# A two-layer mixer network in float32 on one core: loads of x moved to ScalarE's DMA queue, level tables of the recurrent branch made later

## The chip, the cores and the metric

The kernel runs on one core of one Trainium2 chip. The metric is the device time of one execution in microseconds (us); lower is better. The core has five engines that run their own instruction streams in order and meet by semaphores: TensorE (PE, matmuls; its weight loads are listed as PEld), VectorE (DVE), ScalarE (ACT), GpSimd (POOL) and SyncE (SP, which here only issues DMAs). DMAs are also issued from other engines' streams; such an issue stands in that engine's order like any other instruction, with its waits.

## The reference

Two layers over x of 512 rows by 1024 columns, float32. Cut to what matters:

```python
def reference(x, w_in, ..., exp_w1, exp_w3, exp_w2):
    for layer in range(2):
        # p = x @ w_in, split into four branches and a gate:
        # sliding-window attention, RWKV-7 recurrence, forgetting attention, top-k sparse attention
        y = mixer_block(x, w_in[layer], ..., w_branch[layer], w_out[layer])
        x = layer_norm(DN_ALPHA * x + y, ln_g[layer, 0], ln_b[layer, 0])
        if layer == 0:
            y = swiglu(x, ffn_w1[0], ffn_w3[0], ffn_w2[0])
        else:
            y = moe_ffn(x, router_w[0], router_b[0], exp_w1[0], exp_w3[0], exp_w2[0])   # top 2 of 8
        x = layer_norm(DN_ALPHA * x + y, ln_g[layer, 1], ln_b[layer, 1])
    return x

# the recurrent branch, per head (in the kernel: chunks of 64 steps and an inverse of a triangular block)
state = state * w_t + (state @ -kk_t) (x) (kk_t * a_t) + v_t (x) k_t ;  y_t = state @ r_t
```

Each part of `p` and each gate is a projection of x, so before any of them x must be in the chip, transposed, on the contraction axis.

## The kernel before

**How it is tiled.** x is cut into four blocks of 128 rows (`TB = 4`), each in two halves of 512 columns, so x is eight tiles of 128 x 512 (256 KB); below they are x0 to x7. PE transposes each in four 128 x 128 pieces (line 228), ScalarE casts the result to the rounded high part `xh` (line 232) and VectorE subtracts to get the low part `xl` (line 233). Weights come the same way: a 512 KB DMA into `wraw` (two buffers), a ScalarE cast to `whi` (line 98), a VectorE subtraction to `wlo` (line 99; three buffers for each part). Every float32 product is then three matmuls: whi with xh (line 111), whi with xl (line 112), wlo with xh (line 113). An engine's order is fixed when the kernel is built: a scheduler takes instructions by priority, and code under `hot()` or `high_priority()` goes ahead of what stands around it; PSUM tiles have tags (`ps_mm` three buffers; `ps_s`, `ps_t`, `ps_o`, `ps_r`, `ps_y` one each).

**Loads of x.** `load_x` (lines 205 to 212) issues the eight DMAs from SyncE, line 211. It is called four times: at the start; in the merge of layer 0, where x is read again as the residual (about 440 us); at the end of the feed-forward layer (about 830 us); and in the merge of layer 1 (about 1519 us). In the first three the tiles are of the tag `pt`, which has seven buffers, so an eighth load waits until one is read; in the fourth they are of a tag with eight. SyncE's order holds the loads of weights as well (line 322 for `w_in`, 106 for the other matrices, 1382 and the like for the experts' `mwraw`).

**Completion of a DMA.** The scheduler gives every DMA that SyncE or ScalarE issues one of eight completion semaphores in turn, and a DMA waits until the DMA that had its semaphore before has landed. With the loads of x on two issuing engines, these waits cross between SyncE and ScalarE.

**Level tables.** `consts` builds masks on VectorE and GpSimd. Its last part makes `lev`, six masks of 128 x 64 used by the inverse in the recurrent branch (line 863; the uses in the trace start at 158.8 us). It makes integers `iq` and `jq` by shifts (lines 183 to 187), casts them (190, 191), and makes each level in three instructions (195 to 197). These tables lie in a pool that is closed after `consts`; its memory is used again later, among others by the state tiles `SD`, which GpSimd clears (line 804) before it clears a tile and writes it to the scratch buffer `inv` in memory by DMAs (`zero_inv`, lines 727 to 730).

Of the kernel before, what the change touches and what calls it, by code (L numbers as in the profile page):

```python
# [9 lines left out]
F32 = mybir.dt.float32  # L10
F32R = mybir.dt.float32r
BF16 = mybir.dt.bfloat16
I32 = mybir.dt.int32
AF = mybir.ActivationFunctionType
OP = mybir.AluOpType
# [3 lines left out]
P = 128  # L19
# [9 lines left out]
C = 64  # L29
# [27 lines left out]
class Net:  # L57
# [58 lines left out]
    def consts(self, tp):  # L116
        nc, cp = self.nc, self.const
# [50 lines left out]
        for r in range(2):  # L168
            s = self.ident64[64 * r:64 * r + 64]
            nc.gpsimd.affine_select(s, s, pattern=[[1, 64]], base=0, channel_multiplier=-1,  # L170
                                    compare_op=OP.is_equal, fill=0.0)

        self.lev = cp.tile([P, 6, 64], F32, name="lev")
        nc.vector.memset(self.lev, 0.0)
        ii = tp.tile([P, 1], I32, name="ii")
        jj = tp.tile([P, 64], I32, name="jj")
        nc.gpsimd.iota(ii, pattern=[[0, 1]], base=0, channel_multiplier=1)
        nc.gpsimd.iota(jj, pattern=[[1, 64]], base=0, channel_multiplier=0)
        iq = tp.tile([P, 2, 6], I32, name="iq")
        jq = tp.tile([P, 2, 6, 64], I32, name="jq")  # L180
        for l in range(6):

            nc.vector.tensor_scalar(iq[:, 0, l:l + 1], ii, l, 1, op0=OP.logical_shift_right, op1=OP.bitwise_and)
            nc.vector.tensor_scalar(iq[:, 1, l:l + 1], ii, 63, l + 1, op0=OP.bitwise_and,
                                    op1=OP.logical_shift_right)
            nc.vector.tensor_scalar(jq[:, 0, l], jj, l, 1, op0=OP.logical_shift_right, op1=OP.bitwise_and)
            nc.vector.tensor_scalar(jq[:, 1, l], jj, 63, l + 1, op0=OP.bitwise_and, op1=OP.logical_shift_right)
        iqf = tp.tile([P, 2, 6], F32, name="iqf")
        jqf = tp.tile([P, 2, 6, 64], F32, name="jqf")
        nc.vector.tensor_copy(iqf, iq)  # L190
        nc.vector.tensor_copy(jqf, jq)
        t = tp.tile([P, 64], F32, name="levt")
        for l in range(6):

            nc.vector.tensor_scalar(t, jqf[:, 0, l], -1.0, 1.0, op0=OP.mult, op1=OP.add)
            nc.vector.tensor_scalar(t, t, iqf[:, 0, l:l + 1], None, op0=OP.mult)
            nc.vector.scalar_tensor_tensor(self.lev[:, l], jqf[:, 1, l], iqf[:, 1, l:l + 1], t,
                                           op0=OP.is_equal, op1=OP.mult)
        self.reset = cp.tile([P, P], F32, name="reset")
        nc.vector.memset(self.reset, 1.0)  # L200
        nc.vector.memset(self.reset.rearrange("p (c t) -> p c t", t=C)[:, :, 0:1], 0.0)
        self.mhalf = cp.tile([P, 16], F32, name="mhalf")
        nc.vector.memset(self.mhalf, -0.5)


    def load_x(self, src):
        self.x = []
        for tb in range(TB):
            xt = [self.bt(self.xtag), self.bt(self.xtag)]
            for h in range(2):  # L210
                self.nc.sync.dma_start(xt[h], src[tb * P:(tb + 1) * P, h * 512:(h + 1) * 512])
            self.x.append(xt)

    def store_x(self, tb, dst):
# [133 lines left out]
    def mixer(self, layer):  # L348
        self.bp = self.sp
        self.o = {}  # L350
        pr = self.rwkv_proj(layer)
        if layer == 0:
            self.zero_inv()
        with self.hot():
            self.rwkv(layer, pr)
        self.v_proj(layer)
        self.forget()
        for g in range(2):
            q, = self.qk_split(layer, FOX0 + g * P, "qk", 1)
            k = self.dup_split(self.proj_b(layer, (FOX0 + 256 + g * P, P)))  # L360
            self.fox(g, q, k)
        sk = self.dup_split(self.proj_b(layer, (SWA0 + 512, P)))
        for kv in range(2):
            q = self.qk_split(layer, SWA0 + 256 * kv, "qk")
            self.swa(kv, q, sk[kv])
        iq = self.qk_split(layer, DSA0 + 384, "qk")
        k, ik = self.dup_split(self.proj_b(layer, (DSA0 + 256, 64), (DSA0 + 640, 64)))
        masks = self.index(iq, ik)
        self.dsa(self.qk_split(layer, DSA0, "rw"), k, masks)
        self.merge(layer)  # L370
# [1483 lines left out]
```

## Time and profile before

| | |
|---|---|
| Median of 3 runs | 2107.07 us (2104.9 to 2111.75) |
| The profiled execution's own time | 2107.6 us |
| Its span, first to last instruction | 2105.9 us |
| Mean granted TensorE clock | 0.988 of full speed |
| PE busy | 2019.7 us, 96% of the span |
| VectorE, ScalarE, GpSimd busy | 65%, 44%, 7% |

How to read it: a busy share is a mean over stages. PE idles 86.2 us in all (2105.9 - 2019.7), and most of this idle time lies in a few stretches. So the questions to ask of the trace are what PE waited for in the stretch that a change touches, and how long before PE needs it each other engine's result is there. Views used below: busy times of the whole span, busy times by stretches, sums of waits of PE, and timelines (each row: start, duration, engine, line, operation, out <- in, count, and in brackets how long the engine had been idle and what ended that).

### The profile page before, as it was taken

How to read it: one execution, taken by the hardware profiler on the slowest of the kernel's cores; microseconds unless marked ns; L12 is line 12 of the kernel's file. 1: busy time of each engine (PE TensorE's matmuls, PEld its weight loads, DVE VectorE, ACT ScalarE, POOL GpSimd, SP SyncE). 2: the span in 40 equal slices, each digit the busy share in tenths (PEclk: the TensorE clock that was granted, in tenths of full speed). 3: DMA queues.
4: the chain of work that ended last, by engine and by line, in shares of the span. 5: the costliest groups of instructions: out<-in, count | busy, mean ns of one | idle time of the engine just before them, and what ended most of it. 6: DMA issues, size and time to landing. Idle time of an engine off the chain costs nothing. (4 is left out here: it accounts for less than half of the span.)

```text
span 2105.9 us, 31148 instructions
## 1 busy us (share of the span) xinstructions
PE 2019.7 (96%) x11240; PEld 1569.9 (75%) x11240; DVE 1366.6 (65%) x2732; ACT 918.0 (44%) x1561; POOL 151.1 (7%) x211
## 2 busy tenths in 40 slices
PE   8999999999999999999999999999989999999994
PEld 7767777778888888888767778768877766677663
DVE  5677779844563333236676769844568877788778
ACT  3354543333232222113464553332326666677663
POOL 1020200000000000000011200000000000000043
PEclk9999999999999999999999999999999999999997
DMA  5231213343343334233221213313538988898872
GB/s 159 69 84 39 57 41 90 90 125 96 94 146 99 101 93 133 92 98 115 77 58 43 70 41 90 90 51 95 176 128 308 352 291 304 295 342 306 293 280 82
DMA packets 274976, 294.56 MB, mean 140 GB/s; under 512 B 23852, under 2 KB 203416, under 8 KB 274808
## 3 DMA queue, kind: packets, MB, share of 16 engines
q1 hardware_dynamic: 267736, 273.90, 40.2%
q0 software_dynamic: 7072, 18.49, 2.8%
q8 instruction: 97, 1.59, 0.3%
q14 instruction: 71, 0.58, 0.1%
HBM read 276.74 MB, written 15.60 MB: 139 GB/s over the span
## 5 line engine op out<-in xcount | busy, mean ns | idle before, releaser
L98 ACT CAST whi<-wraw 128x1024 fp32r<-128x1024 f32 (+1 forms) x218 | 228.1, 1046 | 625.4 <-PE ps_mm L112 376.9
L99 DVE TENSOR_TENSOR wlo<-wraw,whi 128x1024 fp32r<-128x1024 f32 (+1 forms) x218 | 265.5, 1218 | 361.2 <-ACT whi L98 355.0
L113 PE MATMUL ps_mm<-xh,wlo 128*128 128x512 f32 (+1 forms) x1288 | 494.9, 384 | 3.1 <-DVE rs L259 3.1
L111 PE MATMUL ps_mm<-xh,whi 128*128 128x512 f32 (+1 forms) x1288 | 496.5, 386 | 0.6 <-ACT whi L98 0.5
L112 PE MATMUL ps_mm<-xl,whi 128*128 128x512 f32 (+1 forms) x1288 | 492.1, 382 | 0.3 <-DVE xl L233 0.3
L113 PEld LDWEIGHTS ps_mm<-xh,wlo 128*128 128x128 f32 x1288 | 243.7, 189 | 49.8 <-DVE wlo L99 3.4
L111 PEld LDWEIGHTS ps_mm<-xh,whi 128*128 128x128 f32 x1288 | 243.8, 190 | 46.5 <-issue 2.6
L112 PEld LDWEIGHTS ps_mm<-xl,whi 128*128 128x128 f32 x1288 | 243.7, 189 | 45.8 <-issue 2.3
L1153 DVE TENSOR_TENSOR wlo<-mwraw,whi 128x1024 fp32r<-128x1024 f32 (+1 forms) x98 | 124.2, 1282 | 17.2 <-ACT whi L1152 16.0
L1152 ACT CAST whi<-mwraw 128x1024 fp32r<-128x1024 f32 (+1 forms) x98 | 95.9, 1005 | 16.0 <-PE ps_t L1503 10.1
L470 ACT COPY bt_pt<-ps_t 128x512 f32<-128x512 f32 (+2 forms) x80 | 41.7, 522 | 85.4 <-PE ps_t L467 84.6
L1153 DVE TENSOR_TENSOR mwlo<-mwraw,mwhi 128x1024 fp32r<-128x1024 f32 (+1 forms) x62 | 71.9, 1175 | 6.9 <-ACT mwhi L1152 6.4
L451 ACT ACTIVATE bt_pt<-ps_s,mx 128x256 f32<-128x256 f32 (+3 forms) x128 | 61.8, 487 | 21.8 <-DVE mx L445 18.0
L260 POOL TENSOR_TENSOR rs<-rs,mhalf 128x1 f32<-128x1 f32 x16 | 13.8, 861 | 724.2 <-DVE rs L259 724.2
L442 DVE TENSOR_REDUCE mx<-ps_s 128x2 f32<-128x512 f32 (+3 forms) x80 | 48.5, 607 | 22.1 <-PE ps_s L406 21.1
L1152 ACT CAST mwhi<-mwraw 128x1024 fp32r<-128x1024 f32 (+1 forms) x62 | 61.0, 999 | 3.2 <-DMA mwraw<-in_exp_w_dram 2.3
L1114 DVE TENSOR_TENSOR bt_pt<-bt_pt,ps_mm 128x512 f32<-128x512 f32 x22 | 15.1, 688 | 70.4 <-PE ps_mm L113 63.0
L467 PE MATMUL ps_t<-ident,bt_pt 128*128 128x128 f32 x272 | 51.5, 283 | 6.0 <-DVE bt_pt L461 4.8
L609 DVE MAX8 m<-bt_pt 128x8 f32<-128x256 f32 (+2 forms) x96 | 53.8, 560 | 2.7
L1153 DVE TENSOR_TENSOR wlo<-ring,whi 128x1024 fp32r<-128x1024 f32 (+1 forms) x45 | 51.5, 1160 | 2.5 <-DMA mwraw<-in_exp_w_dram 1.2
L610 DVE MATCH_REPLACE8 bt_pt<-m,bt_pt 128x256 f32<-128x256 f32 (+2 forms) x96 | 52.1, 543 | 0.0
L111 PE MATMUL ps_mm<-bt_o,whi 128*128 128x512 f32 x128 | 51.2, 400 | 0.4 <-ACT bt_o L511 0.4
(710 smaller groups left out, 4119.1 us busy)
## 6 DMA issues: line engine op xcount, KB each, us to landing
mwraw<-in_exp_w_dram SPq DMA_DIRECT2D x124, 512.0 KB
wraw<-in_w_in_dram SPq DMA_DIRECT2D x106, 512.0 KB
wraw<-in_ffn_w_dram SPq DMA_DIRECT2D x66, 512.0 KB
ring<-in_exp_w_dram SPq DMA_DIRECT2D x60, 512.0 KB
wraw<-in_exp_w_dram SPq DMA_DIRECT2D x32, 512.0 KB
mwraw<-in_exp_w_dram SPq DMA_DIRECT2D x36, 384.0 KB
wraw<-in_w_branch_dram SPq DMA_DIRECT2D x20, 512.0 KB
wraw<-in_w_out_dram SPq DMA_DIRECT2D x16, 512.0 KB
```

The costliest lines, as they stand in the source:

```text
L98: nc.scalar.copy(h, src)
L99: (low or nc.vector).tensor_sub(l, src, h.bitcast(F32))
L111: mm(ps, wh, xh, start=start, stop=False)
L112: mm(ps, wh, xl, start=False, stop=False)
L113: mm(ps, wl, xh, start=False, stop=stop)
L442: nc.vector.tensor_reduce(mx[:, 0:nh], s3, op=OP.max, axis=AX.X)
L451: nc.scalar.activation(p3[:, h], s3[:, h], AF.Exp, bias=nm[:, h:h + 1], scale=0.125, accum_out=mx[:, 4 + h:5 + h])
L467: nc.tensor.transpose(pt[:, i * P:(i + 1) * P], p3[:, h, kb * P:(kb + 1) * P], self.ident)
L609: nc.vector.max(m8, sc[:, :nk])
L610: nc.vector.match_replace(sc[:, :nk], m8, sc[:, :nk], REPL)
L1152: self.chain("hi", lambda: nc.scalar.copy(hi[:, :n], src))
L1153: self.chain("lo", lambda: nc.vector.tensor_sub(lo[:, :n], src, hi[:, :n].bitcast(F32)))
```

## The change

It has two parts. In `load_x` the DMA is issued from ScalarE (`nc.scalar.dma_start`) under `hot()`, at all four calls: 32 DMAs leave SyncE's order and stand in ScalarE's. And the part of `consts` that makes the level tables becomes a function of its own, `levels`, called in layer 0 after `rwkv_proj` and `zero_inv`. There `jq` and its float copy lie in four of the 28 buffers of the tag `rw`, and the copy is two casts in place of one. All line numbers from 205 on shift by up to 6.

```diff
@@ consts @@
         self.lev = cp.tile([P, 6, 64], F32, name="lev")
-        nc.vector.memset(self.lev, 0.0)
-        ii = tp.tile([P, 1], I32, name="ii")
-        jj = tp.tile([P, 64], I32, name="jj")
...
-        iq = tp.tile([P, 2, 6], I32, name="iq")
-        jq = tp.tile([P, 2, 6, 64], I32, name="jq")
...
-        nc.vector.tensor_copy(jqf, jq)
...
+    def levels(self):
+        nc = self.nc
+
+        nc.vector.memset(self.lev, 0.0)
+        ii = self.sp.tile([P, 1], I32, name="ii", bufs=1)
+        jj = self.sp.tile([P, 64], I32, name="jj", bufs=1)
...
+        iq = self.sp.tile([P, 2, 6], I32, name="iq", bufs=1)
+        jq = [self.bt("rw", I32)[:, 0:384].rearrange("p (l j) -> p l j", l=6) for _ in range(2)]
...
+        jqf = [self.bt("rw")[:, 0:384].rearrange("p (l j) -> p l j", l=6) for _ in range(2)]
+        nc.vector.tensor_copy(iqf, iq)
+        for a, b in zip(jqf, jq):
+            nc.vector.tensor_copy(a, b)
...
     def load_x(self, src):
...
             for h in range(2):
-                self.nc.sync.dma_start(xt[h], src[tb * P:(tb + 1) * P, h * 512:(h + 1) * 512])
+                with self.hot():
+                    self.nc.scalar.dma_start(xt[h], src[tb * P:(tb + 1) * P, h * 512:(h + 1) * 512])
...
@@ mixer @@
         if layer == 0:
             self.zero_inv()
+            self.levels()
```

ScalarE at the start of the program, before; the names are those of the section above.

```order
L98 ACT_TABLE_LOAD
L98 CAST whi<-wraw 128x1024 x2
L232 CAST xh<-ps_mm 128x4x128
L232 CAST xh<-ps_s 128x4x128
L232 CAST xh<-ps_mm 128x4x128
L98 CAST whi<-wraw 128x1024
L232 CAST xh<-ps_s 128x4x128
```

The same place after the change.

```order
L216 DMA bt_pt<-in_x_dram 128x512 x7
L98 ACT_TABLE_LOAD
L98 CAST whi<-wraw 128x1024 x2
L216 DMA bt_pt<-in_x_dram 128x512
L237 CAST xh<-ps_mm 128x4x128
L237 CAST xh<-ps_s 128x4x128
L237 CAST xh<-ps_mm 128x4x128
L237 CAST xh<-ps_r 128x4x128
L98 CAST whi<-wraw 128x1024
```

Seven loads of x now stand ahead of the table load and of both casts of weights, and the eighth behind these. The seventh waits for the landing of x0, the eighth for that of x1 and for PE's transposes of x0.

TensorE at the start, before.

```order
L228 MATMUL ps_mm<-ident,bt_pt 128x128 x4
L228 MATMUL ps_s<-ident,bt_pt 128x128 x4
L228 MATMUL ps_mm<-ident,bt_pt 128x128 x4
L228 MATMUL ps_r<-ident,bt_pt 128x128 x4
L228 MATMUL ps_s<-ident,bt_pt 128x128 x4
L111 MATMUL ps_mm<-xh,whi 128x256 x2
L112 MATMUL ps_mm<-xl,whi 128x256
```

After.

```order
L233 MATMUL ps_mm<-ident,bt_pt 128x128 x4
L233 MATMUL ps_s<-ident,bt_pt 128x128 x4
L233 MATMUL ps_mm<-ident,bt_pt 128x128 x4
L233 MATMUL ps_r<-ident,bt_pt 128x128 x4
L233 MATMUL ps_y<-ident,bt_pt 128x128
L111 MATMUL ps_mm<-xh,whi 128x256 x2
L233 MATMUL ps_y<-ident,bt_pt 128x128 x2
L233 MATMUL ps_s<-ident,bt_pt 128x128 x4
L233 MATMUL ps_y<-ident,bt_pt 128x128
L112 MATMUL ps_mm<-xl,whi 128x256
```

The first projection's matmuls now have one transpose of x5 (`ps_y`) ahead of them and seven more transposes, of x4 and x5, between the second and the third of them; before, twenty transposes of x0 to x4 stood ahead and those of x5 came later, at 18.10 us.

VectorE, a stretch in the middle of layer 0's projections, after the change: the level tables (lines 194 to 206) among the recurrent branch's preparation (649, 663, 782) and the weights' low parts (99). Before, no level instruction stands there; all lie ahead of line 295, in the first 22 us.

```order
L99 TENSOR_TENSOR wlo<-wraw,whi 128x912
L649 SCALAR_TENSOR_TENSOR bt_rw<-ps_mm,V,bt_rw 128x511
L194 TENSOR_SCALAR bt_rw<-jj 128x64
L195 TENSOR_SCALAR bt_rw<-jj 128x64
L194 TENSOR_SCALAR bt_rw<-jj 128x64
```

Here and in the rest of layer 0's mixer (about 50 to 420 us) the scheduler's order of PE, VectorE and ScalarE differs from before in many places; from there on it is the same but for the next place.

ScalarE in layer 1's merge, before.

```order
L98 CAST whi<-wraw 128x1024 x2
L1152 CAST mwhi<-mwraw 128x1024 x2
L98 CAST whi<-wraw 128x1024 x2
L1230 COPY xT<-ps_mm 128x512
L98 CAST whi<-wraw 128x1024
```

After.

```order
L98 CAST whi<-wraw 128x1024
L216 DMA bt_x<-xs_133 128x512 x8
L1158 CAST mwhi<-mwraw 128x1024
L98 CAST whi<-wraw 128x1024
L1158 CAST mwhi<-mwraw 128x1024
L98 CAST whi<-wraw 128x1024 x2
L1236 COPY xT<-ps_mm 128x512
```

All eight loads of x stand ahead of a cast of weights here, each with its wait for an earlier DMA. Their place in SyncE's order, behind the last `w_out` load, is empty now, and that load, and the constants behind it, wait for landings of x.

GpSimd at the start, after: the four clears of `SD` stand first, and the DMAs of `zero_inv` right behind the mask building, where before both stood behind a wait for the level tables.

## Rows read from the trace of the kernel before

**Rows 1.** The page: busy us, share of the span and instructions of each engine.

```profile
PE 2019.7 (96%) x11240; PEld 1569.9 (75%) x11240; DVE 1366.6 (65%) x2732; ACT 918.0 (44%) x1561; POOL 151.1 (7%) x211
```

**Rows 2.** By stretches: us, each engine's busy us (instructions), PEclk, DMA share, GB/s.

```profile
0.00:12.00 12.00, 5.06 (x22) 4.21 (x23) 8.20 (x46) 5.45 (x7) 3.82 (x21) 1.00 0.90 284
12.00:50.00 38.00, 37.71 (x233) 33.10 (x233) 19.75 (x45) 12.51 (x18) 3.42 (x8) 1.00 0.45 130
50.00:300.00 250.00, 241.07 (x1890) 180.95 (x1889) 176.85 (x535) 126.50 (x319) 34.16 (x51) 1.00 0.23 59
300.00:450.00 150.00, 148.60 (x722) 115.76 (x722) 121.83 (x272) 54.56 (x103) 0.00 (x0) 1.00 0.30 90
1010.00:1400.00 390.00, 376.92 (x2552) 285.71 (x2551) 290.87 (x800) 179.44 (x418) 33.33 (x50) 0.99 0.24 65
1508.00:1525.00 17.00, 17.00 (x76) 13.87 (x74) 8.63 (x22) 5.25 (x5) 1.37 (x7) 1.00 0.86 302
```

**Rows 3.** Waits of PE: who for whom, us in total, times, longest.

```profile
PE ps_mm L228 <- DMA bt_pt<-in_x_dram: 6.7, 1, 6.7
```

**Rows 4.** Line 211 over the whole run: ns min/median/max, first and last start.

```profile
L211 SPq DMA_DIRECT2D bt_pt<-in_x_dram x16: 327/431/1477, 1.9 to 581.7; - x16
```

**Rows 5.** Timeline of SyncE's queue, the start.

```profile
0.81 1.08 SPq L322 DMA_DIRECT2D wraw<-in_w_in_dram  x2
1.94 2.77 SPq L211 DMA_DIRECT2D bt_pt<-in_x_dram  x5
```

**Rows 6.** Timeline of ScalarE, the start.

```profile
0.81 1.28 ACT L98 ACT_TABLE_LOAD   x1 [0.81 <-PEq L1843]
4.46 1.04 ACT L98 CAST whi<-wraw 128x1024 fp32r<-128x1024 f32 x1 [2.36 <-DMA wraw<-in_w_in_dram]
5.95 1.05 ACT L98 CAST whi<-wraw 128x1024 fp32r<-128x1024 f32 x1 [0.45 <-DMA wraw<-in_w_in_dram]
7.87 0.58 ACT L232 CAST xh<-ps_mm 128x512 fp32r<-128x512 f32 x1 [0.88 <-PE ps_mm L228]
...
11.68 1.04 ACT L98 CAST whi<-wraw 128x1024 fp32r<-128x1024 f32 x1 [1.51 <-DMA wraw<-in_w_in_dram]
```

**Rows 7.** Timeline of TensorE, the start.

```profile
6.75 1.09 PE L228 MATMUL ps_mm<-ident,bt_pt 128*128 128x128 f32 x4 [6.75 <-DMA bt_pt<-in_x_dram]
7.63 1.06 PE L228 MATMUL ps_s<-ident,bt_pt 128*128 128x128 f32 x4
...
11.57 0.78 PE L111 MATMUL ps_mm<-xh,whi 128*128 128x256 f32 x2
```

**Rows 8.** Timeline of VectorE, the start.

```profile
9.25 0.68 DVE L233 TENSOR_TENSOR xl<-ps_mm,xh 128x512 fp32r<-128x512 f32 x1
...
21.64 0.29 DVE L197 SCALAR_TENSOR_TENSOR lev<-jqf,iqf,levt 128x64 f32<-128x64 f32 x1
```

**Rows 9.** Timeline of GpSimd, the start.

```profile
22.04 1.06 POOL L804 MEMSET SD<- 128x256 f32 x4 [16.79 <-DVE lev L197]
...
23.88 1.90 POOL L730 DMA_DIRECT2D inv<-bt_rw  x3 [0.31 <-POOL bt_rw L727]
```

**Rows 10.** Timeline of ScalarE, layer 0's merge and the feed-forward's end.

```profile
445.12 0.68 ACT L978 ACTIVATE gate<-ps_mm,V 128x512 f32<-128x512 f32 x1
451.09 1.05 ACT L98 CAST whi<-wraw 128x1024 fp32r<-128x1024 f32 x1 [5.28 <-issue]
...
840.48 1.05 ACT L98 CAST whi<-wraw 128x1024 fp32r<-128x1024 f32 x1 [4.23 <-PE ps_mm L1037]
```

**Rows 11.** Timeline of SyncE's queue, layer 1's merge.

```profile
1513.50 0.37 SPq L106 DMA_DIRECT2D wraw<-in_w_out_dram  x1
...
1519.40 4.78 SPq L211 DMA_DIRECT2D bt_x<-xs  x8
```

**Rows 12.** Timeline of ScalarE, the same stretch.

```profile
1513.76 1.05 ACT L1152 CAST mwhi<-mwraw 128x1024 fp32r<-128x1024 f32 x1 [1.55 <-DMA mwraw<-in_exp_w_dram]
...
1522.04 1.05 ACT L98 CAST whi<-wraw 128x1024 fp32r<-128x1024 f32 x1 [4.43 <-PE ps_mm L1037]
```

More of the change, by code (lines that the diff above doesn't have):

```diff
@@ L173, in consts @@
         self.lev = cp.tile([P, 6, 64], F32, name="lev")
-        nc.vector.memset(self.lev, 0.0)
-        ii = tp.tile([P, 1], I32, name="ii")
-        jj = tp.tile([P, 64], I32, name="jj")
-        nc.gpsimd.iota(ii, pattern=[[0, 1]], base=0, channel_multiplier=1)
-        nc.gpsimd.iota(jj, pattern=[[1, 64]], base=0, channel_multiplier=0)
-        iq = tp.tile([P, 2, 6], I32, name="iq")
-        jq = tp.tile([P, 2, 6, 64], I32, name="jq")
[L181 to L190, printed above, removed]
-        nc.vector.tensor_copy(jqf, jq)
[L192 to L198, printed above, removed]
         self.reset = cp.tile([P, P], F32, name="reset")
@@ L203, in consts @@
         nc.vector.memset(self.mhalf, -0.5)
+    def levels(self):
[3 more added lines that the diff above has]
+        jj = self.sp.tile([P, 64], I32, name="jj", bufs=1)
+        nc.gpsimd.iota(ii, pattern=[[0, 1]], base=0, channel_multiplier=1)
+        nc.gpsimd.iota(jj, pattern=[[1, 64]], base=0, channel_multiplier=0)
+        iq = self.sp.tile([P, 2, 6], I32, name="iq", bufs=1)
+        jq = [self.bt("rw", I32)[:, 0:384].rearrange("p (l j) -> p l j", l=6) for _ in range(2)]
+        for l in range(6):
+            nc.vector.tensor_scalar(iq[:, 0, l:l + 1], ii, l, 1, op0=OP.logical_shift_right, op1=OP.bitwise_and)
+            nc.vector.tensor_scalar(iq[:, 1, l:l + 1], ii, 63, l + 1, op0=OP.bitwise_and,
+                                    op1=OP.logical_shift_right)
+            nc.vector.tensor_scalar(jq[0][:, l], jj, l, 1, op0=OP.logical_shift_right, op1=OP.bitwise_and)
+            nc.vector.tensor_scalar(jq[1][:, l], jj, 63, l + 1, op0=OP.bitwise_and, op1=OP.logical_shift_right)
+        iqf = self.sp.tile([P, 2, 6], F32, name="iqf", bufs=1)
+        jqf = [self.bt("rw")[:, 0:384].rearrange("p (l j) -> p l j", l=6) for _ in range(2)]
+        nc.vector.tensor_copy(iqf, iq)
+        for a, b in zip(jqf, jq):
+            nc.vector.tensor_copy(a, b)
+        t = self.sp.tile([P, 64], F32, name="levt", bufs=1)
+        for l in range(6):
+            nc.vector.tensor_scalar(t, jqf[0][:, l], -1.0, 1.0, op0=OP.mult, op1=OP.add)
+            nc.vector.tensor_scalar(t, t, iqf[:, 0, l:l + 1], None, op0=OP.mult)
+            nc.vector.scalar_tensor_tensor(self.lev[:, l], jqf[1][:, l], iqf[:, 1, l:l + 1], t,
+                                           op0=OP.is_equal, op1=OP.mult)
     def load_x(self, src):
```

## The prediction, made before the change was run

> **What bounds the kernel now.** I read the page's busy times first. TensorE is busy 2019.7 us of the 2105.9 us span, VectorE 65%, ScalarE 44% [rows 1]; so an edit on the other engines moves the time only where it moves one of TensorE's waits. Then the busy times by stretches, to see where TensorE idles near the change [rows 2]. In the first 12 us it works 5.06 and waits 6.94; from 12 to 50 us it waits 0.29; in the rest of layer 0's mixer 250 - 241.07 = 8.93 from 50 to 300 us and 1.40 from 300 to 450 us. Third, the sums of TensorE's waits: loads of x hold it once, for 6.7 us, before its first transpose [rows 3]. The other three calls of `load_x` hold it for nothing. Last, the timelines of the four places where the loads are issued.
>
> So the change can gain at two places only: in the 6.94 us at the start, and in some 10 us of short waits in layer 0's mixer, which it doesn't aim at. At all others it can only lose.
>
> **The start.** Before, SyncE issues two weights, then five tiles of x [rows 5]; they land in that order: the first weight's cast starts at 4.46 us, the second's at 5.95 [rows 6], the first transpose at 6.75 [rows 7], and the third weight, whose issue stands behind the five tiles, is there at 11.68 [rows 6]. The second weight's 512 KB (524,288 bytes) took 5.95 - 4.46 = 1.49 us, 350 GB/s; over the first 12 us the DMA engines were busy 0.90 of the time at 284 GB/s [rows 2]. The loads are therefore held by the transfer of bytes, hardly by SyncE's issue (431 ns at the median, [rows 4]). Issuing x from ScalarE lets x start with the weights instead of behind them, and what one gains the other loses. At stake before the first projection matmul, at 11.57 us [rows 7], are both: it needs x0 and x2 cast, and ScalarE casts both weights before any tile of x, now as before. On top of that its order now has a transpose of x5 ahead of it.
>
> Step by step: the stream of bytes starts at about 4.46 - 1.49 = 3.0 us. If the two queues share evenly, two weights (1.05 MB) have come when as much of x has: 2.1 MB by 350 GB/s is 6.0 us, so the second weight is there at 9.0, not 5.95. Its cast takes 1.05 [rows 6], the eighth load's issue 0.43, three casts of x 0.58 each: 9.0 + 1.05 + 0.43 + 1.7 = 12.2 us. The other limit is x5: weights and six tiles are 2.62 MB, 7.5 us, so 10.5 us; but the four writes of `zero_inv` (1 MB), which now start at about 7 us and not at 23.88 [rows 9], since the wait of 16.79 us for the level tables ahead of them is gone, compete: up to 3.0 us more, 13.5. I take 12.9, the middle of 12.2 and 13.5. Work counts too. Before, twenty transposes stood ahead of the first matmul, now seventeen, and seven follow at once, where before four of these (x5's) came later; at about 0.21 us each (four from 6.75 to 7.63, [rows 7]) that is 3 x 0.21 = 0.6 us on the wrong side if the total is compared at the same point. So 12.9 - 11.57 + 0.6 = **+1.9 us**, and nothing behind it gives it back, since TensorE waits 0.29 us from 12 to 50 us.
>
> The bounds. Below: the weights keep 5.95 (they were issued at 0.81, with nothing before them), casts of x start at 7.4 and x5 lands at 10.5, at best 10.9 - 11.57 + 0.6, about 0. The `jq` shifts are also gone from ahead of the first `xl`, which started at 9.25 [rows 8] though its cast ended at 7.87 + 0.58 = 8.45 [rows 6]: 0.5 of these 0.8 at most, since TensorE had transposes to do. So -0.5. Above: x takes two thirds of the bytes until its seven tiles are there, and `zero_inv` its part: the second weight comes at 11.5, the first matmul at 15, +4.
>
> The Trainium skill (DMA: Bandwidth & Descriptors, section Queues, rings and completion order) says that a DMA engine turns in rotation between the queues that have work for it, a packet at a time, and that SyncE's and ScalarE's queues lie on the same 16 engines. That is the even share above; the trace of before, with one of the two in use, can't show it. By the same page's section Issuing engines are not separate DMA queues, the second issuer saves issue time alone; the rows with 0.90 busy agree.
>
> **The level tables.** Some 45 short instructions leave VectorE's first 22 us. The last ends at 21.93 [rows 8]; the first use is at 158.8 us. TensorE was busy all that time (0.29 us idle from 12 to 50 us), so nothing is saved but the 0.5 above. They go into the projections, where VectorE is 52% busy (19.75 of 38 us, [rows 2]), rising to 71% from 50 to 300 us; the tables cost it about 8 us there (six levels at 0.8 us, casts 0.7, shifts 2.4). Weights are split ahead of TensorE with three buffers for each part, so a delay of 0.3 us per level instruction is covered: 0. If the cover fails, a level or two (0.8 us each) stand ahead of a `wlo` TensorE waits for.
>
> But the scheduler laid out the whole mixer of layer 0 anew. What this does no row shows. The nearest is the same mixer in layer 1, laid out in another order again: it idles 390 - 376.92 = 13.1 us from 1010 to 1400, against 10.3 in layer 0 (8.93 + 1.40). So orders of one mixer differ by some 3 us. I take 0, with -4 to +5 as bounds (half of the idle time gone; one and a half times layer 1's surplus).
>
> **The loads in layer 0's merge and the feed-forward's end.** Eight issues at 0.43 us on ScalarE, 3.4 us. In the merge seven stand ahead of a cast of weights, and one waits for the end of the sparse attention. Replayed against the old times, ScalarE is through with the gate some 1.7 us later than 445.80, and is wanted next at 451.09 after 5.28 us idle [rows 10]. At the feed-forward's end the issues fall into gaps such as the 4.23 us before 840.48 [rows 10]. Both 0; if a landing that ScalarE waits for comes over 3.5 us later than I replay, TensorE waits for the rest.
>
> **The loads in layer 1's merge.** Here they come earlier, in ScalarE's order, and eight stand ahead of a cast of an expert's weights and of the third-last `w_out` cast. The last two of them wait for landings: of the second load of x, and of the first expert weight, which was there at 1513.76 [rows 12] without the competition. TensorE has no idle time there (17.00 of 17 us) and the DMA engines are 0.86 busy at 302 GB/s [rows 2], so 2 MB of x brought forward by some 8 us push others back by up to 2.1 / 0.3 = 7 us. Two things suffer. The `w_out` load issued at 1513.50 [rows 11] now waits for x to land, which I replay to about 1517; TensorE is through with the weight before it near 1522 (the cast at 1522.04 waited for that, [rows 12]). And the last one, before at 1518.99 ahead of x, now stands behind the constants. Against that VectorE may take x as soon as it is in. Cover: ScalarE idles 4.43 us before 1522.04 [rows 12]. A delay of 7 less the cover of 4.4 is 2.6, and part of it is regained as the 4.78 us of issue at 1519.40 [rows 11] is empty: I take **+1**, with -0.5 to +4 (the whole 7 us less half the cover).
>
> **Sum.** 1.9 + 0 + 0 + 1 = +2.9 on the profiled execution's 2107.6 us: 2110.5; it lies 0.5 above the median, so 2110.0. Bounds of all terms in one direction: -5 to +13; I keep the ends that go with one or two terms.
>
> **Rivals.** First, *the gain as meant*: the weights keep their places and x comes with them. For it: the weights are issued no later than now. Against it: bytes, 0.90 busy. -0.5 at the start, 0 to -1 elsewhere: 2106. Second, *the new order of the mixer wins*: 4 to 8 of the 10.3 us go, less the start's loss: 2107.1 - 6 + 1 = 2102, over to 2100 in few cases. For it, that VectorE's and GpSimd's start is free; against, that no wait of the mixer named a level table. Third, on the slower side, *ScalarE's order holds casts behind landings*: the seventh load waits for x0, the last of layer 1 for an expert's weight, while weights ready to be cast stand behind them. Its places are those without cover, the start (+4) and layer 1's merge (+4): 2107.1 + 8 = 2115. It decides from the point at which such a landing is later than 11.5 us at the start, or 1518 in layer 1's merge. Fourth, *the change doesn't do what it says*: x arrives no earlier because the engines, not the issue, set the rate, and no one waits: 2107.
>
> **How the numbers follow.** A measurement of this kernel can tell 0.3%, 6.3 us: 2100.8 to 2113.4 is no change. Forecast (+1 to +6) 0.50; gain as meant 0.12; no effect 0.10; a better mixer 0.12, of which 0.09 under 2100.8; ScalarE held 0.16, of which 0.15 above 2113.4, and 0.03 of the forecast's upper end with it. So faster 0.09, same 0.73, slower 0.18. The range that leaves out about 0.1 on either side is 2102 to 2117.
>
> **What would show it.** Right: the first projection matmul between 12 and 14 us, the second weight's cast near 9, not 5.95; the first transpose before 6; idle time from 50 to 450 us within 7 to 15; TensorE's waits at 440 to 455 and 825 to 960 unchanged; 0 to 4 us of new waits for `whi`, `wlo` or x between 1510 and 1540. Wrong: a first matmul before 11.5 (the queues don't share), idle time in layer 0's mixer under 6 or over 16 us (the order decides), or a cast of weights that ScalarE starts over 4 us late in layer 0's merge.

## The result, and the profile after

The changed kernel takes 2124.13 us at the median of 7 runs (2120.21 to 2128.41), the kernel before 2110.1 us in 7 runs (2104.9 to 2115.41). The ratio is 1.0058, with an interval of 1.0042 to 1.0075: about 12 us slower (the two medians lie 14 us apart). That lies outside the predicted range of 2102 to 2117. The profiled execution took 2124.1 us with a span of 2122.4, 16.5 more than before's; but before's profiled execution, 2107.6, is a low one among its own runs, so the difference of spans says a few us too much.

The page after, busy us of each engine, to be held against [rows 1]:

```profile
PE 2025.9 (95%) x11240; PEld 1571.3 (74%) x11240; DVE 1364.8 (64%) x2733; ACT 916.1 (43%) x1561; POOL 150.9 (7%) x211
```

Of the 16.5 us, 10.3 are idle time of TensorE (96.5 against 86.2) and 6.2 are busy time, with the same 11,240 matmuls. So some matmuls ran more slowly, and the cause of that has to be found as well.

**Where the time goes, by landmarks.** ScalarE casts every weight (`whi`; line 98, for the experts' weights line 1152), in the same number before and after. So I took the n-th such cast in both traces and subtracted the starts; the last column is the first cast of line 1152. The table gives this offset for the changed kernel and for all runs of the experiments below, in us; the first line is the cast's start in the kernel before. The last row is the kernel before, run again: its offsets show what can be read from such a table. They repeat within 0.14 us up to 936 us (0.35 over all casts there) and within 1.2 us up to 1575; behind that, in the mixture of experts, by up to 3.4 us.

| run | projections | 49.5 | end of mixer 0 | merge 0 | feed-forward's end | before merge 1 | behind merge 1 | ratio of times (95%) |
|---|---|---|---|---|---|---|---|---|
| before's start of it | 29.3 | 49.5 | 430.6 | 466.3 | 935.6 | 1500.2 | 1574.9 | |
| after | 4.66 | 4.66 | 2.69 | 12.62 | 12.44 | 12.58 | 15.50 | 1.0058 (1.0042 to 1.0075) |
| levels_only | 6.14 | 6.15 | 4.02 | 3.94 | 3.76 | 4.08 | 6.24 | 1.0004 (0.9994 to 1.0014) |
| loads_only | 3.83 | 12.88 | 17.20 | 26.51 | 26.52 | 26.52 | 32.44 | 1.0114 (1.0097 to 1.0131) |
| merge0_sp | 4.25 | 4.26 | 2.13 | 2.05 | 2.10 | 2.22 | 5.04 | 1.0015 (1.0001 to 1.0028) |
| ln_pool | 5.85 | 5.85 | 5.12 | 7.74 | 7.65 | 7.71 | 10.95 | 1.0038 (1.0023 to 1.0053) |
| merge1_sp | 5.17 | 5.17 | 4.57 | 13.94 | 13.74 | 14.22 | 14.41 | 1.0024 (1.0013 to 1.0035) |
| zinv_late | 4.34 | 4.35 | 2.49 | 11.89 | 11.89 | 12.05 | 14.87 | 1.0054 (1.0035 to 1.0073) |
| xfirst4_b | 2.34 | 9.21 | 9.21 | 9.20 | 9.30 | 10.67 | 10.77 | 1.0031 (1.0019 to 1.0044) |
| xfirst4_l | 1.90 | 7.29 | 6.69 | 6.62 | 6.45 | 5.76 | 5.71 | 1.0011 (1.0002 to 1.0020) |
| x4_b | 3.90 | 3.91 | 4.13 | 4.11 | 3.88 | 4.36 | 4.24 | 1.0026 (1.0013 to 1.0039) |
| x4_l | 6.75 | 6.76 | 6.44 | 6.39 | 6.20 | 7.80 | 7.78 | 1.0003 (0.9985 to 1.0020) |
| levels_zlate | 3.23 | 3.23 | 1.21 | 1.13 | 0.95 | 1.27 | 1.50 | 0.9978 (0.9965 to 0.9992) |
| before_again | 0.14 | 0.14 | 0.09 | 0.09 | -0.10 | 1.14 | 1.10 | 1.0002 (0.9981 to 1.0022) |

The row of the changed kernel is the result in short: 4.7 us lost at the start, 2.0 won in layer 0's mixer, **9.9 lost in layer 0's merge**, nothing at the feed-forward's end, 2.9 lost in layer 1's merge and the routing behind it.

Three cautions on the table. The changed kernel repeats less well than the kernel before: up to 435 us merge0_sp, ln_pool and merge1_sp have the orders of all engines and the completion semaphores of the changed kernel, and yet these four executions lose 4.3 to 5.9 us at the start and win 0.6 to 2.1 in the mixer. So a difference of 1 us there says nothing. Second, in all nine kernels with the tables moved TensorE waits 1.4 us at 73 to 77 us. In ln_pool, merge1_sp, x4_l and xfirst4_l the granted clock fell there to the lower level (1.2 GHz) for 3.4 us, in the other five it did not. The mixer's gain is 0.3 to 0.7 us in the four and 1.9 to 2.1 in the five. Third, in every changed kernel but x4_b the ratio says less loss than the last column, by 2 to 9 us (levels_only 0.8 against 6.2, merge1_sp 5 against 14.4). So against the kernel before at its median they win something back behind 1575 us. Why, no run shows, and the last column does not tell by how much a whole kernel is slower.

The stretches of [rows 2] again, the second and third with their starts moved by the offset (us, busy us of TensorE, its weight loads, VectorE, ScalarE, GpSimd with instructions, granted clock, DMA share, GB/s):

```profile
0.00:12.00 12.00, 4.64 (x17) 3.07 (x17) 3.24 (x19) 3.21 (x3) 7.68 (x30) 1.00 0.88 299
12.00:54.00 42.00, 39.76 (x233) 35.14 (x234) 18.86 (x41) 13.89 (x21) 0.00 (x0) 1.00 0.42 119
54.00:300.00 246.00, 239.14 (x1870) 178.04 (x1869) 178.53 (x557) 125.65 (x317) 31.54 (x49) 1.00 0.23 59
300.00:450.00 150.00, 145.06 (x717) 112.24 (x715) 120.91 (x278) 53.15 (x103) 1.01 (x1) 1.00 0.29 84
```

TensorE idles 7.36 us in the first 12 (6.94 before) and 2.24 in the next 42 (0.29 in 38); 6.86 from 54 to 300 us (8.93 from 50); 4.94 from 300 to 450 (1.40 before), of which 2.96 are the start of the loss in the merge.

The sums of two of TensorE's waits, the first before and after (us in total, times, longest), the second after, where it was 6.7 before [rows 3]:

```profile
PE ps_mm L111 <- ACT bt_o L511: 0.4, 1, 0.4
PE ps_mm L111 <- ACT bt_o L517: 7.3, 2, 7.0
PE ps_mm L233 <- DMA bt_pt<-in_x_dram: 4.8, 2, 4.1
```

### The profile page after: what moved, and what is told of

It is laid out like the page before. It is cut to its first block, busy times and chain, and to the rows that moved or that the text cites. A ratio compares the mean times of both kernels' runs of the same rounds, so it can differ in the third digit from the quotient of the medians.

```text
span 2122.4 us, 31143 instructions
## 1 busy us (share of the span) xinstructions
PE 2025.9 (95%) x11240; PEld 1571.3 (74%) x11240; DVE 1364.8 (64%) x2733; ACT 916.1 (43%) x1561; POOL 150.9 (7%) x211
## 5 line engine op out<-in xcount | busy, mean ns | idle before, releaser
L1159 DVE TENSOR_TENSOR mwlo<-mwraw,mwhi 128x1024 fp32r<-128x1024 f32 (+1 forms) x62 | 71.8, 1174 | 13.0 <-ACT mwhi L1158 12.6
L1158 ACT CAST mwhi<-mwraw 128x1024 fp32r<-128x1024 f32 (+1 forms) x62 | 60.9, 998 | 11.7 <-DMA bt_x<-xs 10.5
```

The costliest lines, as they stand in the source:

```text
L1158: self.chain("hi", lambda: nc.scalar.copy(hi[:, :n], src))
L1159: self.chain("lo", lambda: nc.vector.tensor_sub(lo[:, :n], src, hi[:, :n].bitcast(F32)))
```

## Layer 0's merge: 9.9 us

ScalarE's timeline there, before (start, us, engine, line, operation; in brackets the idle time before it and what ended that):

```profile
443.06 0.27 ACT L511 CAST bt_o<-ps_o 128x128 fp32r<-128x128 f32 x1 [1.41 <-PE ps_o L481]
443.69 0.27 ACT L511 CAST bt_o<-ps_o 128x128 fp32r<-128x128 f32 x1 [0.36 <-DVE bt_o L512]
444.17 1.05 ACT L98 CAST whi<-wraw 128x1024 fp32r<-128x1024 f32 x1 [0.22 <-PE ps_mm L112]
```

And after; the first line is all seven issues, the next two are the fifth of them and the last two:

```profile
443.75 8.38 ACTq L216 DMA_DIRECT2D bt_pt<-in_x_dram  x7
447.27 0.33 ACTq L216 DMA_DIRECT2D bt_pt<-in_x_dram  x1
451.31 0.82 ACTq L216 DMA_DIRECT2D bt_pt<-in_x_dram  x2
452.17 1.04 ACT L98 CAST whi<-wraw 128x1024 fp32r<-128x1024 f32 x1 [7.84 <-DMA bt_pt<-in_x_dram]
453.12 0.68 ACT L984 ACTIVATE gate<-ps_mm,V 128x512 f32<-128x512 f32 x1
453.70 0.26 ACT L517 CAST bt_o<-ps_o 128x128 fp32r<-128x128 f32 x1
```

The seven issues take 8.38 us, not 7 x 0.43 = 3.0. In before the two `bt_o` casts stood ahead of `whi` and the gate; now they stand behind all of it. So the section on the change is wrong where it says that from about 420 us on the orders are the same but for layer 1's merge. The casts are the last branch's output that `w_branch` multiplies, and in TensorE's order its matmuls are next. TensorE after:

```profile
454.01 0.80 PE L111 MATMUL ps_mm<-bt_o,whi 128*128 128x512 f32 x1 [6.97 <-ACT bt_o L517]
...
459.16 0.62 PE L113 MATMUL ps_mm<-xh,wlo 128*128 128x512 f32 x1
459.59 0.43 PE L111 MATMUL ps_mm<-xh,whi 128*128 128x512 f32 x1
459.86 0.40 PE L112 MATMUL ps_mm<-xl,whi 128*128 128x512 f32 x1
460.09 0.39 PE L113 MATMUL ps_mm<-xh,wlo 128*128 128x512 f32 x1
```

The stretch behind the wait, in the columns of [rows 2]:

```profile
454.00:460.00 6.00, 5.99 (x14) 4.46 (x15) 2.34 (x5) 0.27 (x1) 0.00 (x0) 0.53 0.42 123
```

The wait is 6.97 us. Behind it the granted clock is 0.53 (the lower level, 1.2 GHz) until about 459.6, and the matmuls of 512 columns follow each other every 0.43 us instead of 0.23 to 0.24: 13 of them, 13 x 0.19 = 2.5 us more. 7.0 + 2.5 = 9.5 of the 9.9. This is where part of the extra busy time comes from.

What the issues wait for, by the semaphores in the trace: the fifth load of x got the completion semaphore of the first one, which landed at 447.20, and so waited 1.7 us. The sixth got that of the first load of `ln_g` (`bt_v`, a row of 512 numbers spread over 128 partitions), which SyncE issued at 445.05 and which landed at 451.21, 6.2 us later; it waited 3.6 us. The seventh got that of the second load of x, which had landed. The two waits, 5.3 us, are nearly all that the seven issues take over 3.0; the cast of `whi` starts right behind them, at 452.17. Two runs test this. In the first, merge0_sp, the loads of x go back to SyncE at this one place.

```diff
-        self.load_x(self.xsrc)
+        self.load_x(self.xsrc, (layer, which) == (0, 0))     # True: nc.sync, not hot
```

> The changed kernel, but the eight loads of x of layer 0's merge issued from SyncE. Theory: the wait of 7.0 us for the cast of the sparse attention's output and the half clock behind it go away, 9.8 us in all: 6 to 7 us over the kernel before. Rival (the merge's stall has another cause, such as the end of the sparse attention in its new order): the stall stays, or under 4 us go.

Offset at the end of the mixer 2.13, behind the merge 2.05: the whole 9.9 us are gone, and the time is 1.0015 of before's (1.0001 to 1.0028), some 3 us over it and not the 6 to 7 expected. ScalarE has the `bt_o` casts at 445.18 and 445.80 again, ahead of `whi` at 446.27.

The second run, ln_pool, leaves the loads of x on ScalarE and moves the four broadcast loads to GpSimd's queue, so that they hold no semaphore that a load of x can be given. The orders of TensorE, VectorE and ScalarE are those of the changed kernel.

```diff
-                nc.sync.dma_start(t[h], self.I[n][layer, which:which + 1, ...
+                (nc.gpsimd if (layer, which) == (0, 0) else nc.sync).dma_start(t[h], ...
```

> The changed kernel, but the four loads of the normalization's vectors in layer 0's merge issued from GpSimd's queue, which has completion semaphores of its own; the orders of TensorE, VectorE and ScalarE stay the same. Theory: ScalarE is held because its sixth load of x has the semaphore of the first of these vectors' loads and waits until it has landed (7.0 us from issue to landing at the median), and a cast of weights and the cast of the sparse attention's output stand behind it. Then the gap of 7.8 us on ScalarE falls to 1 to 3 us, and 7 to 9.8 us of the loss go. Rival: the loads hold ScalarE by their own landings or by the competition for the DMA engines: the gap stays over 5 us.

ScalarE in this run:

```profile
446.18 3.31 ACTq L216 DMA_DIRECT2D bt_pt<-in_x_dram  x7
449.52 1.04 ACT L98 CAST whi<-wraw 128x1024 fp32r<-128x1024 f32 x1 [2.77 <-PE ps_mm L113]
451.05 0.26 ACT L517 CAST bt_o<-ps_o 128x128 fp32r<-128x128 f32 x1
```

The issues take 3.31 us, near the prediction's 0.43 each, and the merge loses 2.6 us (5.12 to 7.74); the clock does not fall there. The orders are the same, so the waits for landings, with the lower clock that followed, make 7.3 of the 9.9 us, and 2.6 come from the order alone: issues, `whi` and gate ahead of `bt_o`. In this run all seven loads of x have semaphores of their own, so both waits are gone; it does not tell the 1.7 us for x from the 3.6 for `ln_g`. That the start lost 1.2 us more here is chance: its orders and semaphores are those of the changed kernel.

## The start: 4.7 us

ScalarE after, beside [rows 6]:

```profile
0.81 3.58 ACTq L216 DMA_DIRECT2D bt_pt<-in_x_dram  x7
6.26 1.04 ACT L98 CAST whi<-wraw 128x1024 fp32r<-128x1024 f32 x1 [0.56 <-DMA wraw<-in_w_in_dram]
11.12 1.04 ACT L98 CAST whi<-wraw 128x1024 fp32r<-128x1024 f32 x1 [3.81 <-DMA wraw<-in_w_in_dram]
```

The first weight came 1.8 us later than before, the second 5.2 (5.95 to 11.12; I had put it at 9.0). The DMA view gives each queue's packets, MB and share of the 16 engines; q10 holds ScalarE's loads of x, q1 SyncE's weights, q0 GpSimd's writes of `zero_inv`. The first two lines are from 0 to 6.3 us, the others from 6.3 to 11.2:

```profile
q10 hardware_dynamic: 401, 0.75, 38.1%
q1 hardware_dynamic: 1236, 0.62, 33.5%
q10 hardware_dynamic: 607, 1.09, 59.2%
q1 hardware_dynamic: 844, 0.42, 28.7%
q0 software_dynamic: 108, 0.39, 19.4%
```

Until the first weight was there x had 55% of the bytes; from then until the second it had 57%, `zero_inv` 20% and the weight 22%. Of what the two queues of loads moved by 11.2 us (2.88 MB), x took 64%, near the two thirds of the prediction's upper bound. The Trainium skill (DMA: Bandwidth & Descriptors, section Queues, rings and completion order) says that an engine turns between the queues a packet at a time. It gives a packet no fixed size, so the even share of bytes was the prediction's own step and not the page's; no run here shows the turning itself. TensorE after, beside [rows 7]:

```profile
4.06 1.09 PE L233 MATMUL ps_mm<-ident,bt_pt 128*128 128x128 f32 x4 [4.06 <-DMA bt_pt<-in_x_dram]
...
10.70 0.42 PE L233 MATMUL ps_y<-ident,bt_pt 128*128 128x128 f32 x1
13.68 0.58 PE L111 MATMUL ps_mm<-xh,whi 128*128 128x256 f32 x1 [2.55 <-ACT xh L237]
16.21 0.56 PE L112 MATMUL ps_mm<-xl,whi 128*128 128x256 f32 x1
...
19.13 0.37 PE L113 MATMUL ps_mm<-xh,wlo 128*128 128x256 f32 x1
19.34 0.28 PE L111 MATMUL ps_mm<-xh,whi 128*128 128x256 f32 x1
19.46 0.28 PE L112 MATMUL ps_mm<-xl,whi 128*128 128x256 f32 x1
```

The first transpose starts 2.7 us earlier, and it helps nothing. The first projection matmul comes 2.1 us later (11.57 to 13.68), the first with `xl` 4.06 later (12.15 to 16.21), with four more transposes done by then (0.85 us): 3.2 us. And then the matmuls of 256 columns go every 0.21 us until 19.3, where before this pace ended at 12.57. The clock column shows 1.00 in both, but only because it counts what has no record as full speed: the trace holds no clock record before 19.33 us, nor that of before any before 12.64. And 0.21 per 256 columns is the pace of the rows at 0.53 above (0.43 per 512). Fifteen matmuls at 0.21 in place of 0.12 are 1.3 us more. 3.2 + 1.3 = 4.5, of 4.66 measured.

Whether the writes of `zero_inv`, now at 6.67 instead of 23.88 us [rows 9], took bytes from the weights (I had allowed them up to 3.0 us) was tested in zinv_late by one instruction of GpSimd that makes them wait for the constants `V`, to 28.15 us; all other engines keep the order.

```diff
         self.nc.gpsimd.memset(z, 0.0)
+        self.nc.gpsimd.tensor_scalar(z[:, 0:64], self.V, 0.0, None, op0=OP.mult)
```

> The changed kernel with the writes of zero_inv held back until the vectors' transposes (about 27 us) by one small GpSimd instruction; the orders of TensorE, VectorE, ScalarE and SyncE are those of the changed kernel. Theory: x, whose rows are 2 KB, takes more of the bytes than the weights, whose rows are 512 bytes, so the second weight comes late with or without zero_inv: its cast stays near 11 us and the start's loss near 4 us. Rival: zero_inv's 1 MB takes the bytes: the cast comes near 9 us and the loss at the start falls to 1 to 2.5 us.

The second cast comes at 11.17 us and the start loses 4.35. The changed kernel's own start, in four executions, has this cast at 11.12 to 12.20 us and loses 4.3 to 5.9. So the rival, a cast near 9 us, is out, and no cost of `zero_inv` is seen; one under about 1 us would not be. What the writes had taken went to the third weight instead, which landed at 12.63 us and not at 15.61, and for which TensorE waited in neither run. The time is 1.0054 of before's (1.0035 to 1.0073), that of the changed kernel.

Would fewer tiles on ScalarE's queue help? Here only x0 to x3 of the first load go by ScalarE, all other loads by SyncE, without (x4_b) and with (x4_l) the moved tables.

```diff
+                if first and tb < 2:
+                    with self.hot():
+                        self.nc.scalar.dma_start(xt[h], ...)
+                    continue
                 self.nc.sync.dma_start(xt[h], ...
```

> The kernel before, with x0 to x3 of the first load alone issued from ScalarE, where none of the four waits for anything; all other orders are those of before but for a few matmuls. Theory: issuing x beside the weights takes bytes from them and nothing is won: 2.1 MB must land before both weights are cast, the second cast starts at 8.5 to 10 us, the first projection matmul between 11.6 and 12.8 us, 0 to 1.5 us are lost in all. Rival, the gain as meant: the first matmul comes before 11.2 us and 0.5 us or more are gained.

> The same four loads on ScalarE, with the level tables moved. In this order ScalarE's cast of the third weight stands ahead of those of x2 and x3, as it does with all loads on SyncE. Theory: that order makes the loss at the start: first matmul at 13.5 us or later, 4 to 6 us lost by 30 us, 2 us regained in layer 0's mixer. Rival: with x0 to x3 there early the start loses under 2 us, and the kernel is no slower than the kernel before.

In the first, the second weight comes at 9.04, as early as the bytes of two weights and four tiles allow (2.1 MB), but 3.9 us are lost all the same; the time is 1.0026 of before's (1.0013 to 1.0039). I had overlooked VectorE:

```profile
10.12 1.23 DVE L99 TENSOR_TENSOR wlo<-wraw,whi 128x1024 fp32r<-128x1024 f32 x1 [1.40 <-ACT whi L98]
...
12.34 0.68 DVE L237 TENSOR_TENSOR xl<-ps_mm,xh 128x512 fp32r<-128x512 f32 x1
```

and TensorE of the same run:

```profile
13.90 1.11 PE L232 MATMUL ps_s<-ident,bt_pt 128*128 128x128 f32 x4 [3.04 <-DVE xl L237]
```

The cast of x0 ended at 10.57, but its `xl` stood behind the second `wlo` and eleven short shifts of the tables, and the next transposes wait for the buffer that the second `xl` frees; the first matmul comes at 14.66, not by 12.8 as expected. With the tables moved it is 6.8 us lost at the start, more than the 4 to 6 expected, with 0.3 and not 2 us won back in the mixer (the lower clock at 76 us), and yet a time not to be told from before's, 1.0003 (0.9985 to 1.0020).

## Each part alone

My first theory was that the loads of x cost everything and the tables nothing. One part at a time:

```diff
 # levels_only: the changed kernel, but in load_x
-                with self.hot():
-                    self.nc.scalar.dma_start(xt[h], ...)
+                self.nc.sync.dma_start(xt[h], ...)
 # loads_only: the kernel before, but in load_x
-                self.nc.sync.dma_start(xt[h], ...)
+                with self.hot():
+                    self.nc.scalar.dma_start(xt[h], ...)
```

> Level tables moved as in the change, all loads of x issued from SyncE as before. Theory: the three losses of the change (4.65 us at the start, 9.8 in layer 0's merge, 3.7 in layer 1's merge and routing, by landmarks in the two traces) all come from the loads, and the 2.0 us gained in layer 0's mixer from the level tables' move. Then this kernel ends about 2 us below the kernel before, with TensorE's idle time up to 54 us at about 7. Rival: the early writes of zero_inv, which come with the level tables, make part of the loss at the start: then 1 to 2 us are lost up to 30 us here too.

> Loads of x issued from ScalarE as in the change, level tables made at the start as before. Theory: the loads cost it all: 4 to 4.7 us at the start, 9.8 in layer 0's merge, 3.7 in layer 1's, and layer 0's mixer gains nothing, so 17 to 18 us over the kernel before. Rival (part of the start's loss comes with zero_inv's early writes): 2 to 3 us at the start, 15 to 16 in all.

The theory fell. The offsets at 1500 us are 4.1 with the tables alone, 26.5 with the loads alone and 12.6 with both: the parts don't add, since the scheduler lays out the start anew for each and different stalls come of it. By the whole time the tables alone cost nothing that can be told (1.0004), the loads alone 1.0114.

With the tables alone the start loses 6.1 us. ScalarE's order now has the third weight's cast ahead of that of x2, and this weight landed at 12.5 us:

```profile
12.54 1.04 ACT L98 CAST whi<-wraw 128x1024 fp32r<-128x1024 f32 x1 [3.20 <-DMA wraw<-in_w_in_dram]
14.13 0.79 PE L111 MATMUL ps_mm<-xh,whi 128*128 128x256 f32 x2 [2.82 <-ACT xh L236]
17.35 1.12 PE L232 MATMUL ps_y<-ident,bt_pt 128*128 128x128 f32 x4 [2.43 <-DMA bt_pt<-in_x_dram]
```

The mixer behind it wins 2.1 us (6.15 to 4.02), as in the changed kernel (2.0). The kernels that keep the tables at the start win nothing there (0.0 and -0.2 in xfirst4_b and x4_b). So the mixer's gain is the tables' new order, and the prediction had left it at 0.

With the loads alone another stall appears at 30 to 45 us, of 9.0 us:

```profile
37.34 1.04 ACT L98 CAST whi<-wraw 128x1024 fp32r<-128x1024 f32 x1 [3.17 <-DMA wraw<-in_w_in_dram]
38.30 1.84 ACT L643 ACTIVATE bt_rw<-ps_mm,V 128x512 f32<-128x512 f32 x3
...
40.45 0.77 PE L111 MATMUL ps_mm<-xh,whi 128*128 128x512 f32 x1 [4.28 <-DVE bt_rw L644]
...
40.00:50.00 10.00, 9.54 (x20) 6.03 (x21) 1.62 (x3) 0.76 (x2) 0.00 (x0) 0.52 0.20 54
214.00:224.00 10.00, 10.00 (x46) 7.32 (x43) 5.19 (x16) 4.53 (x14) 1.30 (x2) 0.51 0.11 18
```

The order has three weight casts ahead of three activations of the recurrent branch, which must read PSUM before TensorE can go on; the third weight is late, and the clock is 0.52 for the ten us behind. Merge 0 costs 9.3 again. Another 4.2 us go between 186 and 218 us by before's times, and there the granted clock is 0.51 for ten us (last line). TensorE's waits there, 0.88, 0.35 and 0.49 us, stand in the kernel before too, where the clock stayed at 1.00; so these 4.2 us go with the lower clock and with no new wait.

Then levels_zlate, which is levels_only with the line of zinv_late that makes `zero_inv` wait:

> Level tables moved, all loads on SyncE, and the writes of zero_inv held back to about 27 us; ScalarE's order, with the cast of the third weight ahead of x2's, stays. Theory: half of the 6.1 us that the level tables' move costs at the start is that order, half the bytes of zero_inv, which delay the third weight (12.54 us against 11.68) and x5 (17.35 us): the loss falls to 2 to 3.5 us, and the whole kernel ends within 1 us of the kernel before. Rival: the order alone does it, and the loss stays over 5 us; or zero_inv alone, and it falls under 1 us.

The third weight came at 11.91 instead of 12.54, the first matmul at 13.49, and the transposes of x5 at 14.22 instead of 17.35:

```profile
13.49 0.51 PE L111 MATMUL ps_mm<-xh,whi 128*128 128x256 f32 x2 [2.03 <-ACT xh L236]
14.22 1.09 PE L232 MATMUL ps_y<-ident,bt_pt 128*128 128x128 f32 x4 [0.22 <-DMA bt_pt<-in_x_dram]
```

The start loses 3.2 us instead of 6.1. So here, with all of x on one queue behind the weights, the early writes do take about what the prediction feared, 2.9 us, through x5, and the rest is left to the order; it is one execution of each. This kernel is the only one with a lower time than the kernel before: 2108.15 us against 2112.78 of the kernel before, 0.9978 (0.9965 to 0.9992). That is 0.2%, no more than the interval which the kernel before shows against itself (0.9981 to 1.0022). Where it gains is open: up to 1575 us its landmarks lie 1.5 us behind before's, so the gain must come from the stretch behind, where the executions of one kernel differ by several us.

Last, what the change was after, an early x, by another way: x0 to x3 issued ahead of all weights, on SyncE, without (xfirst4_b) and with (xfirst4_l) the moved tables.

```diff
-                self.nc.sync.dma_start(xt[h], ...)
+                with self.hot() if first and 2 * tb + h < 4 else ExitStack():
+                    self.nc.sync.dma_start(xt[h], ...)
```

> The kernel before with x0 to x3 ahead of the first two weights in SyncE's own order, and nothing on ScalarE's queue; behind the first projections all orders are those of before. Theory: the start is held by which bytes come first and by the order of the casts, not by the issuing engine: first transpose near 4 us, first projection matmul between 10.5 and 11.5 us with four more transposes done, 0.5 to 2 us gained in all. Rival: moving bytes within a full stream gains nothing, since weights come later by as much: within 0.5 us, or a loss of 1 to 3 us from casts in a new order.

> The same order of x0 to x3 and the weights on SyncE, with the level tables moved as in the change. Theory: layer 0's mixer keeps its gain of 2 us; the start doesn't have the cast of the third weight ahead of those of x2 and x3, and loses at most 2 us to the early writes of zero_inv: -2 to +1 us against the kernel before. Rival: the level tables' move costs 4 us or more at the start whatever the order of x.

The first transpose starts at 3.75 us, and yet 2.3 us are lost at the start (1.9 with the tables moved), since the second weight comes at 10.14. Then both run into the stall of three weight casts ahead of three activations, 6.9 and 5.4 us more. The times are 1.0031 (1.0019 to 1.0044) and 1.0011 (1.0002 to 1.0020); a gain of 0.5 to 2 us had been expected of the first. In no run did an earlier first transpose bring anything: the first projection needs weights and x, and what x gained the second weight lost, which came at 9.0 to 12.2 us wherever x went ahead of it or beside it, and at 5.95 before.

## Layer 1's merge: 2.9 us

ScalarE after, beside [rows 12]:

```profile
1521.63 8.22 ACTq L216 DMA_DIRECT2D bt_x<-xs  x8
1529.89 1.05 ACT L1158 CAST mwhi<-mwraw 128x1024 fp32r<-128x1024 f32 x1 [10.55 <-DMA bt_x<-xs]
...
1539.40 1.06 ACT L98 CAST whi<-wraw 128x1024 fp32r<-128x1024 f32 x1 [5.61 <-DMA wraw<-in_w_out_dram]
...
1544.83 1.05 ACT L98 CAST whi<-wraw 128x1024 fp32r<-128x1024 f32 x1 [3.89 <-DMA wraw<-in_w_out_dram]
```

Eight issues again take 8.22 us. The last two weights come late: the load of the first waits for the buffer that a cast held on ScalarE frees (issue at 1533.36), and that of the second stands behind the constants in SyncE's order (1540.59). TensorE waits 0.7 us for VectorE's `bt_x` and 0.7 for the router's weights: 1.4 of the 2.9; the rest, spread over the routing, I did not trace. The run merge1_sp sends x by SyncE at this place alone:

```diff
+        self.load_x(self.xsrc, (layer, which) == (1, 0))     # True: nc.sync, not hot
```

> The changed kernel, but the eight loads of x of layer 1's merge issued from SyncE. Theory: all that the changed kernel loses behind 1505 us comes from their place ahead of casts of weights: 3 to 4 us are saved, about 12.5 over the kernel before remain. Rival: the loss there is from another start of the experts' part: under 1 us saved.

The offset from 1500.2 to 1574.9 goes from 14.22 to 14.41, so 0.2 us are lost in place of 2.9, and TensorE is busy for 59.95 of the 60 us from 1500 to 1560. The time is 1.0024 of before's (1.0013 to 1.0035), less than the landmarks alone would give; behind 1575 us it must have won something back, which stays open like the gain of levels_zlate.

The kernel before, run again as a case of its own (before_again), set the measure for all offsets:

> The kernel before once more, for a second profile: how far landmarks differ between two executions of one program. Theory: up to the experts' part (about 1570 us) they agree within 1 us, so that differences of 2 us and more between kernels there are the kernels'; behind it, where the DMA engines are 0.85 busy, they differ by several us. Rival: they differ by 2 us or more already in the first 450 us, and then the terms read from landmarks can't be told from chance.

Its ratio is 1.0002 (0.9981 to 1.0022).

## Why the prediction was wrong, by its steps

- **The start**: mechanism right, size wrong. Predicted +1.9 with -0.5 to +4, measured +4.7. The mis-sized term is the second weight, 11.12 us in place of 9.0, as x took 64% of the bytes of the loads and not half. A term was missing: matmuls at half pace until 19.3 us, 1.3 us. The term for x5 behind `zero_inv`, up to 13.5 us, was not needed: x5's first transpose came at 10.70, as its bytes alone gave (10.5).
- **The level tables**: predicted 0 with -4 to +5, measured -2.0 in the mixer, in five executions, and -0.3 to -0.7 in the four with the lower clock at 73 to 77 us. Their absence from the start, taken as a gain of 0.5 at most, changes the order there: alone they cost 6.1 us at the start.
- **Layer 0's merge**: this step failed, 0 predicted and +9.9 measured. It put ScalarE's next need at 451.09 [rows 10] and so found 5.3 us of cover. But the `bt_o` casts, which TensorE needs at about 447, were moved behind the issues too, and I listed only `whi` and the gate as standing there. And my replay had ScalarE through with the gate 1.7 us late; it was 5.3 late (453.80, less the offset of 2.69, against 445.80), as one issue waited 1.7 us for the first load of x and one 3.6 for `ln_g`. The rival that had just this mechanism named the start and layer 1's merge as its places, not this one. The 2.5 us at half clock had no term. What failed is the path: no term had TensorE wait for `bt_o` behind the issues.
- **The feed-forward's end**: 0 predicted. The offset goes from 12.62 to 12.44. Right.
- **Layer 1's merge**: +1 predicted with -0.5 to +4, +2.9 measured. Right in kind, and inside its bounds, though 1.5 of it were not traced to a wait.
- **The working**: two bounds don't come out of their own terms. Half of the mixer's 10.3 us is 5.2 and one and a half times layer 1's surplus of 2.8 is 4.2, so -5 to +4 and not -4 to +5; 7 less half of 4.4 is 4.8, not 4. Neither would have moved the range to 2124. The base, the median of three runs (2107.07), lay 3 us under that of seven (2110.1).
- **The signs named in advance**: first matmul between 12 and 14 us (13.68: seen), first transpose before 6 (4.06: seen), second weight near 9 (11.12: not), idle time from 50 to 450 us within 7 to 15 (11.8 from 54 on: seen), TensorE's waits at 440 to 455 unchanged (not), those from 825 to 960 (seen), up to 4 us of new waits between 1510 and 1540 (0.7 for x: seen), and "a cast of weights that ScalarE starts over 4 us late in layer 0's merge" as the sign that the prediction is wrong (452.17 against 444.17, 8 us, and 5.3 less the offset: seen).

With the merge at its measured 9.9 us, and all else as predicted, the forecast would have been 2120; with the start's 4.7 as well, about 2123. That this comes so near 2124 is partly luck: the mixer's -2.0 and layer 1's +1.9 over its term cancel, the base was 3 us low, and what the kernels win behind 1575 us has no term at all.

## What to carry to other kernels

A DMA issued from a compute engine is an instruction of that engine: write down everything that stands behind it there, not only the next one, and for each the time at which someone needs it; then give the issue the longest landing in the trace that it can be made to wait for, by way of completion semaphores also that of a DMA which another engine issued. A wait of TensorE can cost more than its length: behind 6.97 us the matmuls ran at the lower clock for 5.6 us, and at a wait of 1.4 us the clock fell in four of nine executions, so one profile doesn't tell whether it will. And two edits whose order a scheduler chooses can't be priced apart and added.

## What was not expected of the hardware

- After 6.97 us without a matmul TensorE's granted clock was 0.53 for some 5.6 us: 2.5 us on top of the wait. At a wait of 1.4 us it fell for 3.4 us in four of nine executions, among them two of four that had the same orders. In loads_only it fell for ten us among waits of under 0.9 us, which cost 4.2 us; in the kernel before, with the same waits, it stayed.
- At the start the matmuls ran at the half pace, 0.21 us per 256 columns, until 19.3 us, where the trace has no clock record and the column shows 1.00.
- Two loads of one row spread over 128 partitions (256 KB) took 6.2 and 7.0 us to land beside the loads of x.
- x, issued on ScalarE's queue beside two weights on SyncE's, took 55% of the bytes until the first weight was there, and 57% from then until the second, when the weight got 22% and `zero_inv` 20%.
- Up to 936 us, two executions of the kernel before set the same cast within 0.35 us, where the time as a whole spreads over ten. Four executions of the changed kernel's start differ by 1.6 us. So single profiles compare to tenths of a us only where the kernel's own repetition has shown it.
